# First attention block of a four-block transformer kernel: shift and scale computed in blocks of columns, and the first six projections accumulated side by side

## Chip, core and metric

One NeuronCore of a Trainium2 chip runs the whole kernel; the other cores are idle. The metric is the time of one execution in microseconds (us), taken as the median of several runs. The engines are called PE (TensorE), DVE (VectorE), ACT (ScalarE), POOL (GpSimd) and SP (SyncE, which here only issues DMAs); PEld is the loading of PE's weights.

## What is computed

The reference has four residual blocks on 1024 tokens of width 1024, in float32. Only the first is touched. Cut to what matters:

```python
mod = jax.nn.silu(c) @ ada_w[0] + ada_b[0]              # c: (1,1024), ada_w[0]: (1024, 3072)
shift, scale, gate = jnp.split(mod[:, None, :], 3, axis=-1)
u = x * (1 + scale) + shift                             # (1,1024,1024)
q, k, v, gate = jnp.split(u @ w_in, 4, axis=-1)         # w_in: (1024, 4*1152), 18 heads of 64
for g, (window, dil) in enumerate(((128, 1), (512, 4), (2048, 16))):   # 6 heads per group
    s = q k^T * 64**-0.5 + bias[t5_bucket(rel * dil)]   # masked to the dilated window
    o, lse = softmax(s) v, logsumexp(s)
y = concat(o * softmax(lse over the three groups)) * silu(gate)
x = layernorm(ALPHA * x + mod_gate * (y @ w_out))
```

Nothing can be projected before `u` is there, and a feature column of `u` needs its own shift and scale, each a product of all 1024 entries of silu(c) with one column of `ada_w`.

## The kernel before

Every float32 matrix product is made of three passes with two-part numbers: an operand is split into a rounded part `h` and a remainder `l`, and PE adds up w_l·u_h, w_h·u_h and w_h·u_l (`PASSES`). The input of a block stands transposed, by feature tiles of 128 (`kt`, eight of them) and by halves of 512 tokens (`h`): `uh0`, `ul0`, `uh1`, `ul1` (class `UT`). A projection of 128 output columns for one half of the tokens takes 8 x 3 = 24 matmuls of 512 columns into one PSUM bank.

`phase_A` is the first block. Its beginning, lines 341 to 427, goes through these steps:

- The vector `c` is loaded, turned, and passed through silu (`cs`). Four tiles of `x` (128 tokens each) are loaded on ACT's queue, then the one-hot table `oh` and `rel_bias`, from which PE forms three rows of attention biases (`tvs`). PE transposes the four `x` tiles and ACT copies them to `xT0` (`turn_x`).
- DVE forms silu(c)·ada_w for all 2048 columns of shift and scale: 16 loads of `ada_w` (128 rows x 1024 columns, in rows of 4 KB) go through the five `raw` buffers, and each is weighted by one column of `cs` and added to `acc` (lines 396 and 398).
- The first three weight tiles of `w_in` (`load_w`: columns of q, k and v for the first pair of heads) follow in SP's queue and are split on DVE. PE adds `acc` over the partitions with 16 matmuls against `cz` (32 instructions) and one transpose. `mc` then holds all 16 columns of shift and 1 + scale.
- Only now is `u` formed: per feature tile and half, DVE computes `xm`, ACT `uh`, and DVE or POOL `ul` (lines 418 to 422). The other four tiles of `x` are loaded on SP's queue behind the weights and turned.
- Three bias rows are written to DRAM and read back spread over 128 partitions (`tvd`, `tbd`), later loaded as the shifted tables `T`.

Then the groups follow. `dil_project` for the first group runs its six products (q, k, v by two halves) one after the other, each 24 matmuls into a bank of `g` or `t`, with `q`, `k` and `kl` split off PSUM by ACT and DVE while PE goes on. `dil_batches` forms the jobs of a head (ten per pair of heads): scores on PE, bias, maximum on DVE, exponential on ACT, transposes on PE (`t`), a split on ACT (`pth`) and DVE (`ptl`), and values on PE. Between the transposes and the values of a job PE is given pieces of the next group's projections (`fill`). `mod_jobs` meanwhile forms the other four slices of shift, scale and gate for later use: a load of `ada_w` and a weighing on DVE (`weigh`, line 552) per job.

The order on each engine is set by the Tile scheduler, except where `keep_in_program_order` or `self.pin` fixes it. Each engine runs its own list in order. SP's list holds nearly all DMA issues; one that waits for a buffer holds up all behind it.

Of the kernel before, what the change touches and what calls it, by code (L numbers as in the profile page):

```python
# [12 lines left out]
F32 = mybir.dt.float32  # L13
F32R = mybir.dt.float32r
I32 = mybir.dt.int32
AF = mybir.ActivationFunctionType
# [5 lines left out]
P = 128  # L22
S = 1024
D = 1024
# [117 lines left out]
class Kern:  # L142
    def __init__(self, nc, tc, ins, out):
        self.nc, self.tc, self.i, self.out = nc, tc, ins, out
        self.n = 0
        self.ready = {}
        self.pin = False
        self.ps = Pools(None, {})
# [6 lines left out]
    def tr(self, *args):  # L155
        ins = self.nc.tensor.transpose(*args)  # L156
        if self.pin:
            self.tc.keep_in_program_order(ins)

    def nm(self, s):  # L160
# [46 lines left out]

    def load_w(self, pool, w, c0, n, kts=KT, tag="w", bufs=None, dve=0, cut=1):

        nc = self.nc  # L210
        step = min(kts, max(1, 1024 // n))
        res = []
        kw = {} if bufs is None else {"bufs": bufs}
        for k0 in range(0, kts, step):
            m = min(step, kts - k0)
            r = self.raw([P, step, n])
            nc.sync.dma_start(r[:, :m], w[k0 * P:(k0 + m) * P, c0:c0 + n].rearrange("(k p) n -> p k n", p=P))
# [114 lines left out]
    def phase_A(self, x_in):  # L332
        nc, i = self.nc, self.i
        with ExitStack() as ctx:
            self.wp = self.tags(ctx, "wp", bufs=3)
# [5 lines left out]
            with ExitStack() as c0:  # L341
                tp = self.tags(c0, "a0", side="right")
                self.psum(c0, "", "mx")
                c8 = tp.tile([P, KT], F32, name="c8")
                self.transposed_columns(c8, i["c"].rearrange("o (k p) -> (o k) p", p=P), KT, tp)
                self.silu2(cs, c8, cs)
                nc.vector.tensor_scalar(cs, cs, 0.5, None, OP.mult)
                xT = [tp.tile([P, KT, 512], F32, name=f"xT{h}") for h in range(2)]

                def load_x(t):  # L350
                    xts[t] = tp.tile([P, D], F32, tag="xt", bufs=4, name=self.nm("xt"))
                    return (nc.sync if t > 3 else nc.scalar).dma_start(xts[t], x_in[t * P:(t + 1) * P, :])

                def turn_x(t):
                    xt = xts[t]
                    for h in range(2):
                        ps = self.pp("x", 3, [P, 4, P])
                        self.transposes(ps, xt[:, h * 512:(h + 1) * 512], 4)
                        dst = xT[t // 4][:, h * 4:h * 4 + 4, t % 4 * P:(t % 4 + 1) * P]
                        nc.scalar.copy(dst, ps)  # L360

                xts = {}
                for t in range(4):
                    load_x(t)

                oh = tp.tile([33, 3, 512], F32, name="oh")
                nc.scalar.dma_start(oh, i["k_onehot"])
                rb = tp.tile([33, 18], F32, name="rb")
                nc.vector.memset(rb[32:33, :], NEG)
                nc.scalar.dma_start(rb[:32, :], i["rel_bias"])  # L370
                tvs = []
                for g in range(3):
                    ps = self.pp("x", 3)
                    self.mm(ps[:6, :], rb[:, g * 6:(g + 1) * 6], oh[:, g, :], start=True, stop=True)
                    tvs.append(tp.tile([6, 512], F32, tag="tv", bufs=3, name=self.nm("tv")))
                    nc.scalar.copy(tvs[g], ps[:6, :])
# [5 lines left out]
                nc.vector.tensor_scalar(mc[:, 8:], mc[:, 8:], 1.0, None, OP.add)  # L382
                for t in range(4):
                    turn_x(t)

                cz = tp.tile([P, 256], F32, name="cz")
                nc.gpsimd.memset(cz, 0.0)
                nc.gpsimd.tensor_copy(cz[:, ::17], self.ones.to_broadcast([P, 16]))
                acc = tp.tile([P, 2, 1024], F32, name="acc")
                for kt in range(KT):  # L390
                    for j in range(2):
                        r = self.raw()
                        self.tc.keep_in_program_order(nc.sync.dma_start(
                            r, i["ada_w"][0, kt * P:(kt + 1) * P, j * 1024:(j + 1) * 1024]))
                        if kt == 0:
                            nc.vector.tensor_scalar(acc[:, j], r, cs[:, 0:1], None, OP.mult)
                        else:
                            nc.vector.scalar_tensor_tensor(acc[:, j], r, cs[:, kt:kt + 1], acc[:, j], OP.mult, OP.add)
                for c0 in (0, WA, 2 * WA):
                    self.ready[c0] = self.load_w(self.wp, i["a_w_in"][0], c0, P, dve=1 - c0)  # L400
                mp = self.pp("m", 1, [16, P])
                for c in range(16):
                    self.mm(mp, cz[:, c * 16:c * 16 + 16], acc[:, c // 8, c % 8 * P:(c % 8 + 1) * P],
                            start=(c == 0), stop=(c == 15))
                row = tp.tile([16, P], F32, name="row")
                nc.vector.tensor_copy(row, mp)
                mt = self.pp("t", 2)
                self.tr(mt[:, :16], row, self.ident[:16, :16])
                nc.vector.tensor_tensor(mc, mc, mt[:, :16], OP.add)
                for t in range(4, NT):  # L410
                    self.tc.keep_in_program_order(load_x(t))
                for h in range(2):
                    if h:
                        for t in range(4, NT):
                            turn_x(t)
                    for kt in range(KT):
                        xm = tp.tile([P, 512], F32, tag="xm", bufs=4, name=self.nm("xm"))
                        nc.vector.tensor_scalar(xm, xT[h][:, kt], mc[:, 8 + kt:9 + kt], mc[:, kt:kt + 1], OP.mult, OP.add)
                        nc.scalar.activation(ut.hi[h][:, :, kt], xT[h][:, kt], AF.Identity,
                                             bias=mc[:, kt:kt + 1], scale=mc[:, 8 + kt:9 + kt])  # L420
                        eng = nc.gpsimd if kt % 3 == 2 else nc.vector
                        eng.tensor_tensor(ut.lo[h][:, :, kt], xm.rearrange("p (t n) -> p t n", n=P),  # L422
                                          ut.hi[h][:, :, kt].bitcast(F32), OP.subtract)
                for g in range(3):
                    nc.sync.dma_start(tvd[g * 6:(g + 1) * 6, :], tvs[g])
                    nc.sync.dma_start(tbd[g * 6:(g + 1) * 6],
                                      tvd[g * 6:(g + 1) * 6, None, :].to_broadcast([6, P, 512]))
            c1 = ExitStack()
            self.psum(c1, "", "so")
            ag = self.tags(ctx, "ag")  # L430
# [18 lines left out]
            self.order += [gate_w(2, g) for g in range(3)]  # L449
            for n, _ in enumerate(fills[0]):  # L450
                self.pin = n >= 5
            mods = self.mod_jobs(lp, cs, ((0, 2), (1, 0), (1, 1), (1, 2)))
# [147 lines left out]
    def dil_project(self, lp, ut, w_in, hp, g, res):  # L600
# [15 lines left out]

        def project(c, h, evac, tag):
            w = self.next_w(c)
            self.next_w(c, 1)
            ps = self.pp(tag, 2)  # L620
# [39 lines left out]
        first = hp + g == 0  # L660
        order = [(j, h) for h in range(2) for j in range(3)]
        for j, h in order if first else sorted(order):
            yield from project(j * WA + c0, h, evacs[j], "t" if first and (j, h) == (2, 0) else "g")
        vh = lp.tile([P, NT, P], F32R, tag="vh", bufs=2, name=self.nm("vh"))
# [1241 lines left out]
```

## Time and profile before

| | |
|---|---|
| median of 3 runs | 4132.61 us (4131.44 to 4135.64) |
| the profiled execution | 4131.9 us |
| its span in the trace | 4130.1 us |
| PE busy with matmuls | 3858.2 us, 93% of the span |
| DVE, ACT, POOL busy | 59%, 33%, 26% |
| first of the 144 matmuls of the first six projections | starts at 39.80 us |
| last of them | starts at 75.72 us |
| first matmul of the second group's projections | starts at 77.53 us |

All times are from the start of the span. The span is 1.8 us shorter than the execution's own time. The last three lines of the table are read from the timeline of PE. A line such as "x<-ident,xt" names what an instruction writes and reads; "[idle before <-DVE acc]" is the time that the engine stood still ahead of it and what ended it.

### The profile page before, as it was taken

Reading aid. Unit: us, or ns where it says so; the run is one execution under the profiler, and the core shown is the slowest. Engines: PE = TensorE matmul, PEld = TensorE weight load, DVE = VectorE, ACT = ScalarE, POOL = GpSimd, SP = SyncE. Lnnn points to the kernel's source line nnn. Section 1 sums busy time; section 2 is a strip of 40 time slices with the busy share of each in tenths; the row PEclk is TensorE's granted clock in tenths of the full one; section 3 lists DMA queues with packets and bytes.
Section 4 is the critical chain, followed back from the end, with each engine's and each line's share of the span. In section 5 each row is a group of like instructions: output and inputs, shape, how many; then the busy total and the mean of one; then the engine's idle time right before and its main releaser. Section 6 shows DMA issues by size and latency. Waiting matters only on the chain. (4 is left out here: it accounts for less than half of the span.)

```text
span 4130.1 us, 54373 instructions
## 1 busy us (share of the span) xinstructions
PE 3858.2 (93%) x21085; PEld 3272.8 (79%) x21085; DVE 2447.7 (59%) x4596; ACT 1382.1 (33%) x2938; POOL 1085.5 (26%) x1016
## 2 busy tenths in 40 slices
PE   7979796899999989999999999997999999999998
PEld 5767675688889867999778888885999778888886
DVE  6645455956777767568754434338568764443436
ACT  3424242124777633256421111113136431111111
POOL 1111111420222322134233232334134232323233
PEclk9989898999999989999999999998999999999999
DMA  6363516220111243111421111113111231111112
GB/s 237 96 82 83 76 41 149 95 86 29 35 25 32 62 120 117 41 38 37 137 83 48 45 51 41 51 50 120 55 42 37 95 115 46 47 46 51 41 51 82
DMA packets 318897, 290.80 MB, mean 70 GB/s; under 512 B 70779, under 2 KB 273267, under 8 KB 318638
## 3 DMA queue, kind: packets, MB, share of 16 engines
q1 hardware_dynamic: 313362, 268.23, 23.5%
q10 hardware_dynamic: 5276, 19.08, 1.5%
q8 instruction: 167, 2.74, 0.3%
q14 instruction: 92, 0.75, 0.1%
HBM read 240.26 MB, written 51.72 MB: 71 GB/s over the span
## 5 line engine op out<-in xcount | busy, mean ns | idle before, releaser
L203 POOL TENSOR_TENSOR wl<-wr,wh 128x1024 fp32r<-128x1024 f32 (+1 forms) x253 | 495.4, 1966 | 1589.6 <-DVE wh L199 1502.8
L199 DVE CAST wh<-wr 128x1024 fp32r<-128x1024 f32 x222 | 181.9, 820 | 751.7 <-PE y L151 310.7
L151 PE MATMUL y<-uh_m,wl 128*128 128x512 f32 x1056 | 417.1, 395 | 4.7 <-DVE z L1631 4.2
L151 PE MATMUL y<-uh_m,wh 128*128 128x512 f32 x1056 | 419.8, 398 | 0.0
L151 PE MATMUL y<-ul_m,wh 128*128 128x512 f32 x1056 | 418.8, 397 | 0.0
L1784 ACT ACTIVATE cv<-y,cw 128x1024 f32<-128x1024 f32 x66 | 79.8, 1209 | 775.7 <-PE y L151 775.7
L151 PE MATMUL g<-uh_a,wl 128*128 128x512 f32 x568 | 236.8, 417 | 55.2 <-DVE sg L293 55.1
L151 PEld LDWEIGHTS y<-uh_m,wl 128*128 128x128 f32 x1056 | 199.0, 188 | 55.1 <-issue 4.6
L151 PEld LDWEIGHTS y<-uh_m,wh 128*128 128x128 f32 x1056 | 199.1, 189 | 48.4
L151 PEld LDWEIGHTS y<-ul_m,wh 128*128 128x128 f32 x1056 | 198.9, 188 | 47.6 <-DVE ul_m L191 0.9
L151 PE MATMUL y<-wo,yh 128*128 128x512 f32 x784 | 219.8, 403 | 17.0 <-ACT yh L1158 17.0
L151 PE MATMUL g<-ul_a,wh 128*128 128x512 f32 x568 | 229.3, 404 | 0.5 <-POOL ul_a L422 0.4
L151 PE MATMUL g<-uh_a,wh 128*128 128x512 f32 x568 | 228.7, 403 | 0.0
L151 PEld LDWEIGHTS y<-wo,yh 128*128 128x128 f32 x784 | 149.2, 193 | 50.7 <-ACT yh L1158 18.5
L191 DVE TENSOR_TENSOR pt<-t,pt 128x512 fp32r<-128x512 f32 x256 | 165.8, 680 | 22.2 <-ACT pt L190 20.4
L151 PE MATMUL y<-wl,hh 128*128 128x512 f32 x440 | 175.4, 399 | 0.0
L151 PE MATMUL y<-wh,hl 128*128 128x512 f32 x440 | 175.1, 398 | 0.0
L151 PE MATMUL y<-wh,hh 128*128 128x512 f32 x440 | 175.1, 398 | 0.0
L151 PEld LDWEIGHTS g<-uh_a,wl 128*128 128x128 f32 x568 | 111.5, 196 | 78.9 <-DVE sg L293 49.5
L995 DVE TENSOR_REDUCE nm<-s 128x1 f32<-128x1024 f32 x128 | 155.7, 1216 | 27.1 <-PE s L151 26.5
L151 PE MATMUL g<-wl,uh_f 128*128 128x256 f32 x576 | 166.4, 289 | 3.0 <-DVE dv L191 2.5
L151 PE MATMUL g<-wl,uh_n 128*128 128x256 f32 x576 | 166.0, 288 | 3.1 <-DVE dv L191 2.5
(446 smaller groups left out, 10312.2 us busy)
## 6 DMA issues: line engine op xcount, KB each, us to landing
wr<-w_up SPq DMA_DIRECT2D x88, 512.0 KB
wr<-ada_w SPq DMA_DIRECT2D x48, 512.0 KB
wr<-w_down SPq DMA_DIRECT2D x44, 512.0 KB
wr<-a_w_in SPq DMA_DIRECT2D x36, 512.0 KB
wr<-w_in SPq DMA_DIRECT2D x24, 512.0 KB
xs<-wr SPq DMA_DIRECT2D x16, 512.0 KB
wr<-xs ACTq DMA_DIRECT2D x16, 512.0 KB
wr<-w_in SPq DMA_DIRECT2D x32, 256.0 KB
```

The lines of the kernel that those rows point to most:

```text
L151: ins = self.nc.tensor.matmul(*args, **kw)
L191: nc.vector.tensor_tensor(lo, src, hi.bitcast(F32), OP.subtract)
L199: (self.nc.scalar.copy if act else self.nc.vector.tensor_copy)(hi, raw)
L203: (eng or self.nc.gpsimd).tensor_tensor(lo[..., cs], raw[..., cs], hi[..., cs].bitcast(F32), OP.subtract)
L995: nc.vector.tensor_reduce(nm, sp, AX.X, OP.max, negate=True)
L1784: nc.scalar.activation(t, ps, AF.Identity, bias=cw[:, 3, c:c + 1], scale=cw[:, 2, c:c + 1])
```

## The change

The beginning is written anew. Shift and scale come in four blocks of columns: block `pr` holds shift and scale of the two feature tiles 2·pr and 2·pr+1. `load_mod(pr)` loads it with eight DMAs (rows of 1 KB) into four of six new buffers `ra`; `mod(pr)` weighs it on DVE in eight steps of 512 columns, adds it over the partitions on PE with four one-column matmuls and puts it into `mc`; `modulate(kt, h)` makes `uh` and `xm` both on ACT and `ul` on DVE. `product(j, h, kts)` adds some feature tiles to projection j, half h. The six projections stand in six PSUM banks (`g`, two, and `x`, four), so that a feature tile can be added to all six as soon as it is there. The banks of the scores (`s`, `o`) are opened only after the six banks of the first group have been read (`cx.close()`). `chain` fixes the order of an engine's listed instructions; with `pin` the first three weight tiles are rounded on ACT and not on DVE.

```diff
+    def chain(self, ins):
+        prev = self.last.get(ins.ins.engine)
+        if prev:
+            self.tc.add_manual_dep(ins.ins, prev, ...)
+        self.last[ins.ins.engine] = ins.ins.name
...
-            self.wsplit(hi[:, :m], lo[:, :m], r[:, :m], eng, cut)
+            self.wsplit(hi[:, :m], lo[:, :m], r[:, :m], eng, cut, pin)
...
-                self.psum(c0, "", "mx")
+                self.psum(cx, "", "x")
+                def load_mod(pr):
+                    cols = i["ada_w"][0, :, 0:2048].rearrange("(k p) (a n) -> p k a n", p=P, a=2)
+                    rows[pr] = []
+                    for k in range(0, KT, 2):
+                        r = tp.tile([P, 2, 2, 256], F32, tag="ra", bufs=6, name=self.nm("ra"))
+                        for a in range(2):
+                            self.chain(
+                                nc.sync.dma_start(r[:, :, a], cols[:, k:k + 2, a, pr * 256:(pr + 1) * 256]))
+                        rows[pr].append(r)
+                def mod(pr):
+                    acc = tp.tile([P, 2, 256], F32, tag="acc", bufs=2, name=self.nm("acc"))
+                    for k in range(KT):
+                        r = rows[pr][k // 2][:, k % 2]
+                        self.chain(nc.vector.tensor_scalar(acc, r, cs[:, 0:1], None, OP.mult) if k == 0 else
+                                   nc.vector.scalar_tensor_tensor(acc, r, cs[:, k:k + 1], acc, OP.mult, OP.add))
+                    ps = self.pp("t", 2)[:, :4].rearrange("p (a k) -> p a k", a=2)
+                    for a in range(2):
+                        for k in range(2):
+                            self.mm(ps[:, a, k:k + 1], acc[:, a, k * P:(k + 1) * P], self.ones, start=True, stop=True)
+                    m = mc.rearrange("p (a k) -> p a k", a=2)[:, :, 2 * pr:2 * pr + 2]
+                    self.chain(nc.vector.tensor_tensor(m, m, ps, OP.add))
+                def modulate(kt, h):
+                    xm = tp.tile([P, 512], F32, tag="xm", bufs=3, name=self.nm("xm"))
+                    nc.scalar.activation(ut.hi[h][:, :, kt], xT[h][:, kt], AF.Identity,
+                                         bias=mc[:, kt:kt + 1], scale=mc[:, 8 + kt:9 + kt])
+                    nc.scalar.activation(xm, xT[h][:, kt], AF.Identity, bias=mc[:, kt:kt + 1], scale=mc[:, 8 + kt:9 + kt])
+                    self.chain(nc.vector.tensor_tensor(ut.lo[h][:, :, kt], xm.rearrange("p (t n) -> p t n", n=P),
+                                                       ut.hi[h][:, :, kt].bitcast(F32), OP.subtract))
+                for t in range(2):
+                    load_x(t, nc.scalar)
...
+                for t in (2, 3):
+                    load_x(t, nc.sync)
+                load_mod(0)
...
+                for t in range(4):
+                    turn_x(t)
+                for j in range(3):
+                    ws.append(self.load_w(self.wp, w_in, j * WA, P, dve=int(j == 1), pin=True))
+                mod(0)
+                for t in range(4, NT):
+                    load_x(t, nc.sync)
+                load_mod(1)
+                for kt in range(2):
+                    modulate(kt, 0)
+                for kt in range(2):
+                    for j in range(3):
+                        product(j, 0, [kt])
+                for t in range(4, NT):
+                    turn_x(t)
+                mod(1)
+                for kt in range(2):
+                    modulate(kt, 1)
+                load_mod(2)
+                for kt in range(2):
+                    for j in range(3):
+                        product(j, 1, [kt])
+                for kt in (2, 3):
+                    for h in range(2):
+                        modulate(kt, h)
+                mod(2)
+                load_mod(3)
+                for kt in (2, 3):
+                    for h in range(2):
+                        for j in range(3):
+                            product(j, h, [kt])
+                for kt in (4, 5):
+                    for h in range(2):
+                        modulate(kt, h)
+                mod(3)
+                for kt in (6, 7):
+                    for h in range(2):
+                        modulate(kt, h)
...
+                for kt in (4, 5):
+                    for h in range(2):
+                        for j in range(2):
+                            product(j, h, [kt])
+                for j, h in ((0, 0), (1, 0), (0, 1), (1, 1), (2, 0), (2, 1)):
+                    product(j, h, range(6 if j < 2 else 4, KT))
```

The first place is DVE's list from the second to the fourth block of columns. Here `acc` is the weighing of a block, `mc` the sum that completes its shift and scale, and `ul_a` the remainder of a feature tile, for which the two results of ACT (`xm`, `uh_a`) must be there. In the change:

```order
L392 TENSOR_TENSOR mc<-mc,t_376 128x2x2
...
L399 TENSOR_TENSOR ul_a<-xm_435,uh_a 128x4x128
L385 TENSOR_SCALAR acc_439<-ra_390,cs 128x512
L386 SCALAR_TENSOR_TENSOR acc_439<-ra_390,cs,acc_439 128x512
L386 SCALAR_TENSOR_TENSOR acc_439<-ra_393,cs,acc_439 128x512 x2
L386 SCALAR_TENSOR_TENSOR acc_439<-ra_396,cs,acc_439 128x512 x2
L386 SCALAR_TENSOR_TENSOR acc_439<-ra_399,cs,acc_439 128x512 x2
L392 TENSOR_TENSOR mc<-mc,t_448 128x2x2
L399 TENSOR_TENSOR ul_a<-xm_502,uh_a 128x4x128
...
L385 TENSOR_SCALAR acc_518<-ra_454,cs 128x512
```

Each block's weighing stands behind the last `ul_a` of the block before it (six of them ahead of `acc_439`, four ahead of `acc_518`). Before, all the weighing comes first, then one `mc`:

```order
L398 SCALAR_TENSOR_TENSOR acc<-wr_268,cs,acc 128x1024
L199 CAST wh_276<-wr_271 128x1024
...
L409 TENSOR_TENSOR mc<-mc,t_317 128x16
L418 TENSOR_SCALAR xm_331<-xT_111,mc 128x512
L418 TENSOR_SCALAR xm_335<-xT_111,mc 128x512
L418 TENSOR_SCALAR xm_339<-xT_111,mc 128x512
L422 TENSOR_TENSOR ul_a<-xm_331,uh_a 128x4x128
```

The second place is DVE's list in the eighth and ninth of the ten jobs of the first group. Here `xs`, `stats` and `ptl` are a job's biased scores, maximum and split remainder; `wr<-wr,cs,wr` is a weighing of `mod_jobs`. Before:

```order
L762 SCALAR_TENSOR_TENSOR xs_1075<-s_1070,T_715 128x512
L191 TENSOR_TENSOR ptl_1086<-t_1080,pth_1085 128x512
L769 TENSOR_REDUCE stats_717<-xs_1075 128x2
L552 SCALAR_TENSOR_TENSOR wr_760<-wr_1067,cs,wr_760 128x1024
L762 SCALAR_TENSOR_TENSOR xs_1128<-s_1123,T_715 128x512
L769 TENSOR_REDUCE stats_717<-xs_1128 128x2
L191 TENSOR_TENSOR ptl_1139<-t_1133,pth_1138 128x512
```

In the change:

```order
L829 TENSOR_REDUCE stats_743<-xs_1101 128x2
L609 SCALAR_TENSOR_TENSOR wr_786<-wr_834,cs,wr_786 128x1024
L609 SCALAR_TENSOR_TENSOR wr_786<-wr_881,cs,wr_786 128x1024
L609 SCALAR_TENSOR_TENSOR wr_786<-wr_931,cs,wr_786 128x1024
L207 CAST wh_952<-wr_950 128x1024
L609 SCALAR_TENSOR_TENSOR wr_786<-wr_1001,cs,wr_786 128x1024
L609 SCALAR_TENSOR_TENSOR wr_786<-wr_1046,cs,wr_786 128x1024
L207 CAST wh_1117<-wr_1115 128x1024
L609 SCALAR_TENSOR_TENSOR wr_786<-wr_1093,cs,wr_786 128x1024
L822 SCALAR_TENSOR_TENSOR xs_1154<-s_1149,T_741 128x512
L829 TENSOR_REDUCE stats_743<-xs_1154 128x2
L199 TENSOR_TENSOR ptl_1165<-t_1159,pth_1164 128x512
```

Six weighings and two roundings of weights now stand in a row between the eighth job's maximum and the ninth job's scores; before, the six were spread over the third to the ninth job. On PE the two lists are the same, instruction for instruction, from the first group's v transposes to the end; on DVE, ACT, POOL and SP they are the same from the tenth job of the first group.

## Rows read from the trace of the kernel before

**Rows 1.** The page's first part: busy us, share of the span, instructions.
```profile
PE 3858.2 (93%) x21085; PEld 3272.8 (79%) x21085; DVE 2447.7 (59%) x4596; ACT 1382.1 (33%) x2938; POOL 1085.5 (26%) x1016
```
**Rows 2.** Windows: engines' busy us, then granted clock, DMA share, GB/s.
```profile
0.00:4.00 4.00, 0.24 (x1) 0.18 (x1) 0.30 (x3) 0.00 (x0) 1.11 (x8) 1.00 0.54 150
4.00:8.00 4.00, 0.28 (x1) 0.18 (x1) 0.68 (x4) 1.49 (x2) 0.00 (x0) 1.00 1.02 418
8.00:12.00 4.00, 0.00 (x0) 0.00 (x0) 1.50 (x2) 0.00 (x0) 0.00 (x0) 1.00 1.03 370
12.00:16.00 4.00, 1.51 (x2) 0.24 (x3) 2.03 (x2) 0.00 (x0) 0.00 (x0) 1.00 1.03 362
...
32.00:36.00 4.00, 4.00 (x24) 2.98 (x23) 3.59 (x4) 0.00 (x0) 0.00 (x0) 0.61 1.15 321
```
**Rows 3.** Timeline of PE: start us, us, instruction [idle before].
```profile
14.48 5.28 PE L151 MATMUL x<-oh,rb 33*6 33x512 f32 x6 [9.44 <-DMA rb<-rel_bias]
19.69 6.24 PE L156 MATMUL x<-ident,xt 128*128 128x128 f32 x32
30.71 5.81 PE L151 MATMUL m<-acc,cz 128*16 128x128 f32 x32 [4.78 <-DVE acc L398]
...
39.80 0.50 PE L151 MATMUL g<-uh_a,wl 128*128 128x512 f32 x1 [0.16 <-ACT uh_a L419]
...
46.95 1.47 PE L156 MATMUL x<-ident,xt 128*128 128x128 f32 x12
```
**Rows 4.** Timeline of PE, end of the first six projections and after.
```profile
75.50 0.39 PE L151 MATMUL g<-uh_a,wh 128*128 128x512 f32 x1
75.72 0.40 PE L151 MATMUL g<-ul_a,wh 128*128 128x512 f32 x1
...
77.53 0.45 PE L151 MATMUL g<-uh_a,wl 128*128 128x512 f32 x1
...
82.60 0.75 PE L156 MATMUL t<-ident,xs 64*128 64x64 f32 x2 [1.63 <-ACT xs L771]
...
84.73 0.63 PE L151 MATMUL g<-uh_a,wl 128*128 128x512 f32 x1
85.16 0.63 PE L151 MATMUL g<-uh_a,wh 128*128 128x512 f32 x1
```
**Rows 5.** Timeline of ACT.
```profile
25.10 1.56 ACT L360 COPY xT<-x 128x512 f32<-128x512 f32 x3 [0.25 <-PE x L156]
...
38.92 5.76 ACT L419 ACTIVATE uh_a<-xT,mc 128x512 fp32r<-128x512 f32 x8
54.69 1.17 ACT L634 CAST q<-g 64x512 fp32r<-64x512 f32 x2
```
**Rows 6.** Groups by line and shape, ACT: count | busy us, mean ns.
```profile
L1797 ACT CAST hh<-cv 128x1024 fp32r<-128x1024 f32 x44 | 46.2, 1049 | 172.8 <-DVE cv L1794 172.8
```
**Rows 7.** Groups by line and shape, 0 to 60 us, DVE.
```profile
L398 DVE SCALAR_TENSOR_TENSOR acc<-wr,cs,acc 128x1024 f32<-128x1024 f32 x14 | 17.9, 1285 | 2.6 <-DMA wr<-ada_w 2.6
...
L422 DVE TENSOR_TENSOR ul_a<-xm,uh_a 128x512 fp32r<-128x512 f32 x12 | 7.9, 682 | 0.1
...
L199 DVE CAST wh<-wr 128x1024 fp32r<-128x1024 f32 x3 | 2.1, 688 | 0.5 <-DMA wr<-a_w_in 0.5
```
**Rows 8.** Timeline of DVE, the first group's splits.
```profile
66.48 1.39 DVE L636 TENSOR_TENSOR q<-g,q 64x512 fp32r<-64x512 f32 x2 [0.52 <-ACT q L634]
71.92 2.81 DVE L647 TENSOR_TENSOR kl<-g,k 64x512 fp32r<-64x512 f32 x4 [4.05 <-ACT k L644]
```
**Rows 9.** Timeline of POOL: splitting the second group's first weights.
```profile
66.04 2.40 POOL L203 TENSOR_TENSOR wl<-wr,wh 128x1024 fp32r<-128x1024 f32 x1 [9.53 <-DVE wh L199]
```
**Rows 10.** Waits, 77 to 135 us: engine <- releaser: us, times, longest.
```profile
PE o L151 <- DVE ptl L191: 3.1, 4, 1.3
...
DVE wh L199 <- DMA wr<-a_w_in: 2.8, 1, 2.8
...
PE o L151 <- ACT pth L190: 1.7, 1, 1.7
```

More of the change, by code (lines that the diff above doesn't have):

```diff
@@ L145, in __init__ @@
         self.n = 0
-        self.ready = {}
+        self.ready, self.last = {}, {}
         self.pin = False
@@ L342, in phase_A, with load_x @@
                 tp = self.tags(c0, "a0", side="right")
-                self.psum(c0, "", "mx")
+                self.psum(cx, "", "x")
+                xT = [tp.tile([P, KT, 512], F32, name=f"xT{h}") for h in range(2)]
+                w_in = i["a_w_in"][0]
+                xts, ws, rows, done = {}, [], {}, set()
+                def load_x(t, eng):
+                    xts[t] = tp.tile([P, D], F32, tag="xt", bufs=4, name=self.nm("xt"))
+                    self.chain(eng.dma_start(xts[t], x_in[t * P:(t + 1) * P, :]))
@@ L344, in phase_A, with product @@
+                def product(j, h, kts):
+                    if (j, h) not in self.first:
+                        self.first[j, h] = self.pp(*(("g", 2) if len(self.first) < 2 else ("x", 4)))
+                    self.gemm_T_half(ws[j], ut, h, self.first[j, h], kts=kts)
+                for t in range(2):
+                    load_x(t, nc.scalar)
                 c8 = tp.tile([P, KT], F32, name="c8")
@@ L347, in phase_A @@
                 nc.vector.tensor_scalar(cs, cs, 0.5, None, OP.mult)
[L348 to L367, printed above, removed]
                 rb = tp.tile([33, 18], F32, name="rb")
                 nc.vector.memset(rb[32:33, :], NEG)
[L370 to L376, printed above, removed]
+                self.chain(nc.scalar.dma_start(rb[:32, :], i["rel_bias"]))
+                oh = tp.tile([33, 3, 512], F32, name="oh")
+                self.chain(nc.scalar.dma_start(oh, i["k_onehot"]))
                 self.ones = self.cp.tile([P, 1], F32, name="ones")
@@ L382, in phase_A @@
                 nc.vector.tensor_scalar(mc[:, 8:], mc[:, 8:], 1.0, None, OP.add)
+                for t in (2, 3):
+                    load_x(t, nc.sync)
+                load_mod(0)
+                self.first = {}
+                self.pin = True
+                tvs = []
+                for g in range(3):
+                    ps = self.pp("t", 2)
+                    self.mm(ps[:6, :], rb[:, g * 6:(g + 1) * 6], oh[:, g, :], start=True, stop=True)
+                    tvs.append(tp.tile([6, 512], F32, tag="tv", bufs=3, name=self.nm("tv")))
+                    nc.scalar.copy(tvs[g], ps[:6, :])
@@ L383, in phase_A @@
                 for t in range(4):
                     turn_x(t)
[L386 to L407, printed above, removed]
@@ L408, in phase_A @@
-                self.tr(mt[:, :16], row, self.ident[:16, :16])
-                nc.vector.tensor_tensor(mc, mc, mt[:, :16], OP.add)
-                for t in range(4, NT):
[L411 to L423, printed above, removed]
@@ L424, in phase_A @@
[L424 to L427 removed]
+                for j in range(3):
+                    ws.append(self.load_w(self.wp, w_in, j * WA, P, dve=int(j == 1), pin=True))
+                    self.ready[j * WA] = ws[j]
+                mod(0)
+                for t in range(4, NT):
+                    load_x(t, nc.sync)
@@ new lines, in phase_A @@
+                for g in range(3):
+                    self.chain(nc.sync.dma_start(tvd[g * 6:(g + 1) * 6, :], tvs[g]))
+                    self.chain(nc.sync.dma_start(
+                        tbd[g * 6:(g + 1) * 6], tvd[g * 6:(g + 1) * 6, None, :].to_broadcast([6, P, 512])))
+                for kt in (4, 5):
+                    for h in range(2):
+                        for j in range(2):
+                            product(j, h, [kt])
+                for j, h in ((0, 0), (1, 0), (0, 1), (1, 1), (2, 0), (2, 1)):
+                    product(j, h, range(6 if j < 2 else 4, KT))
@@ L449, in phase_A @@
             self.order += [gate_w(2, g) for g in range(3)]
-            for n, _ in enumerate(fills[0]):
-                self.pin = n >= 5
+            for _ in fills[0]:
+                pass
+            cx.close()
+            self.psum(c1, "", "so")
             mods = self.mod_jobs(lp, cs, ((0, 2), (1, 0), (1, 1), (1, 2)))
@@ L615, in dil_project, with project @@
         out = res[hp * 3 + g] = []
-        def project(c, h, evac, tag):
+        def project(c, h, evac):
             w = self.next_w(c)
             self.next_w(c, 1)
-            ps = self.pp(tag, 2)
+            if first:
+                evac(h, perm(self.first.pop((c // WA, h))))
+                return
+            ps = self.pp("g", 2)
             for k0 in (0, 4):
@@ L660, in dil_project @@
         first = hp + g == 0
-        order = [(j, h) for h in range(2) for j in range(3)]
+        order = [(0, 0), (1, 0), (0, 1), (1, 1), (2, 0), (2, 1)]
         for j, h in order if first else sorted(order):
-            yield from project(j * WA + c0, h, evacs[j], "t" if first and (j, h) == (2, 0) else "g")
+            yield from project(j * WA + c0, h, evacs[j])
         vh = lp.tile([P, NT, P], F32R, tag="vh", bufs=2, name=self.nm("vh"))
```

14 lines of the change are left out of this document (11 added, 3 removed).

## Prediction

> **What bounds the kernel now.** Read the page's first part to begin with [rows 1]: PE is busy for 93% of the span, so a delay of PE's own list lasts to the end. From the first group's v transposes on, PE's list is the same in both programs, and nothing later in it is due at a fixed time. So the question is when PE gets there, and what the other engines' lists, which differ as far as the group's tenth job, make it wait for.
>
> Next the windows [rows 2]: from 4 to 16 us the DMA engines are full at 360 to 420 GB/s while PE does next to nothing. Then the timeline of PE [rows 3, 4]: bias rows from 14.48 us, transposes of x, the sum of shift and scale at 30.71, the first projection at 39.80, and 144 matmuls until 75.96 (0.227 us each, from the spacing of the last two), with transposes between. The second group starts at 77.53. Until 39.80 PE has little to do; that is the room the change aims at.
>
> **The change, step by step.** Times are from the start of the span.
>
> *Bias rows.* They wait for the one-hot table behind four x tiles on ACT's queue: 2.3 MB. By 14.48 us both queues have moved 0.6 + 1.67 + 1.48 + 0.9 = 4.65 MB [rows 2], twice 2.3, so they share evenly. Two x tiles fewer leave 1.25 MB, hence 2.5 MB in all: 8.6 us. I take **9**; bounds 7 (the table needs no share) and 11 (the rate falls to 362 GB/s while they land).
>
> *First half of x.* 5.2 us of bias rows, then eight transposes with copies, 19.69 to 26.66 [rows 3, 5]: 7.0. On ACT, three roundings of weights now stand between the copies: 1.05 each [rows 6], of which I take 2.4 as added (none to 3.2). x is ready at **23.6**. Block 1's sums are done by then: its 2.1 MB follow the 2.3 MB of the start, 4.4 MB by 14 us; the weights' 1.6 MB follow by 18.5, in time for their roundings.
>
> *First 18 products.* Two ACT results at 0.72 [rows 5] and one remainder at 0.68 [rows 7] come first: 25.7. Then 16 matmuls: 3.6 us at 0.227. [...] I add 1.7: **31.0**.
>
> [...]
>
> *Second half of x.* Its four loads wait on SP for the buffers of the first four tiles, and block 2's eight loads stand behind them. They are issued between 15 and 22 us and land by 25, hidden. Eight transposes, 6.0 (7.0 at the low level, 5 where only ACT's copies count): xT1 is complete at **37.0**.
>
> *Block 3.* ACT makes 12 results, 8.6 us. The last remainder, 0.7. Only then does DVE weigh block 3, since it stands behind the remainders in its list: one step of 0.4 and seven of 0.64 (half of the 1.285 for twice the columns [rows 7]), 4.9. The sum: four matmuls, two instructions each at 0.18 [rows 3], and the addition, 1.7 (1.1 to 2.5). **52.9**. The loads are there: two blocks, 4.2 MB, in the 25 us since. PE has had 18 products and stands idle from about 42.
>
> *Block 4.* ACT 8 results, 5.8; remainder 0.7; weighing 4.9; sum 1.7: 13.1, so **66.0**. PE's 36 products of feature tiles 2 and 3 take 8.2 and lie inside, low clock included.
>
> *The rest.* 24 products of tiles 4 and 5 and 48 more stand behind block 4's sum in PE's list: 72 x 0.227 = 16.3. ACT's last results (5.8 after the sum) lie under the first 24. PE was idle for some 2 us; after 1.63 us at 82.60 seven matmuls took 0.43 [rows 4], so 1.7 for the clock (0 to 4). **84.0**, against 75.96: **+8.0**.
>
> *Tail.* The second group's first weights are rounded on DVE behind all of q's and k's splits (8.4 us, twice 1.39 and twice 2.81 [rows 8]; they begin 8.3 us before PE's end, since the first product is complete 42 matmuls or 9.5 us before it and ACT needs 1.17 [rows 5]), then 0.7 and POOL's 2.4 [rows 9]: 3.2 after PE's end, where it was 1.6. **+1.6**. The v copies and the later opening of the score banks end about 2 us after PE's end, under that. The tables T come last in SP's list, after block 4; they wait for freed memory until about 72 us and are wanted after 88, so they cost nothing; should they be late, a load and DVE's step.
>
> *Jobs.* Six weighings at 1.28 and two roundings at 0.69 hold DVE for 9.1 us between the eighth and ninth job; with the ninth's scores and maximum the eighth's remainder comes 11.1 us late (bias 0.69, maximum 0.68, split 0.68). PE has about 4.7 us to do meanwhile (exponential, transposes, 12 matmuls). It waits 6.4, up to 9.2 where a weight load lands late as before (2.8 [rows 10]). Gained back: weighings leave the earlier jobs, where PE waited 3.1 for DVE and 1.7 for ACT behind it [rows 10]. I take half of the 3.1, bounds none and 4.8. **+5** (1.6 to 9.2).
>
> *Removed or moved at no cost:* 32 instructions of the old sum on PE and 16 `xm` on DVE lie in the stretch that is rebuilt; POOL's four remainders go to DVE, counted above.
>
> Sum, against the profiled execution's 4131.9 (0.7 under the median of 4132.6, well inside the runs' spread): 4131.9 + 8.0 + 1.6 + 5 = 4146.5, say **4147**. A measurement of this kernel can tell 0.2%, 8.3 us, from no change. The bounds: all low ends together (start -2, roundings -2.4, both clocks -3.4, two sums -1.2, jobs -3.4) give 4134; that they all fall together is unlikely, so 4136. All high ends (start +2, roundings +0.8, clock +2.3, sums +1.6, jobs +4.2) give 4157, and 1.7 more where the long wait among the jobs lowers the clock as that at 82.60 did: 4159.
>
> **Rivals.**
>
> *The jobs lose nothing.* PE would need 11 us of other work between the eighth job's maximum and its values; then the weighings' leaving the earlier jobs counts in full: 4131.9 + 9.6 - 4.8 = 4136.7, no slower than can be told. For it: PE has pieces of projections to fill with. Against: 12 matmuls, 2.7 us, stand there in its list. 13%.
>
> *The blocks overlap after all.* If DVE weighed the next block while ACT works on this one, each block would cost the longer of the two, at most 7.6 (four remainders and a weighing) instead of 13 to 16, and the loads would decide. The 14.2 MB of x, weights and `ada_w` at 370 GB/s end near 40, plus 3 of weighing and sum, plus 16.3: PE done at 60, 16 earlier: 4131.9 - 16 + 1.6 + 5 = 4122.5, faster. It decides once weighing does not wait for remainders; DVE's list says it does. 5%.
>
> [...] 15%.
>
> **Chances.** My forecast 67%, the three rivals 13, 5 and 15%. The forecast's lower end and the first rival make the middle: slower by over 0.2% 0.80, within 0.2% 0.15, faster 0.05. The range 4136 to 4159 holds the forecast with its bounds, the low-clock rival and most of the first.
>
> **What would show it.** In the changed profile: bias rows from about 9 us; DVE's third and fourth block each begin right after a remainder; PE idle for some 10 us before block 3's sum; the last of the six products near 84 and the second group's first matmul near 87; one wait of PE for `ptl` of 6 us or more. Wrong, if PE's first six projections end before 76 us, or if no `ptl` wait passes 3 us.

## The result, and the profile after it

The changed kernel takes 4160.1 us (median of 6 runs, 4158.2 to 4164.1) against 4134.2 us for the kernel before on the same chip: a ratio of 1.0064 (95% interval 1.0051 to 1.0077), so 26 us slower. The forecast was 4147 us, at most 4159. The direction was right and the size too small: the start cost 4 us more than forecast, the jobs three times as much as forecast. The profiled span is 4158.8 us, 28.7 more than before. The page's first part [rows 1] hardly shows it, since PE does the same work:

```profile
PE 3864.8 (93%) x21084; PEld 3277.8 (79%) x21084; DVE 2445.1 (59%) x4597; ACT 1396.9 (34%) x2957; POOL 1083.6 (26%) x1012
```

**The start.** The windows of the changed kernel (columns as in [rows 2]) show PE idle twice, each time with the granted clock down to 0.50 behind it:

```profile
44.00:48.00 4.00, 0.82 (x4) 0.34 (x2) 3.02 (x5) 1.56 (x3) 0.00 (x0) 0.84 0.00 0
48.00:52.00 4.00, 0.00 (x0) 0.00 (x0) 3.82 (x6) 0.00 (x0) 0.00 (x0) 0.50 0.69 215
52.00:56.00 4.00, 3.66 (x13) 3.30 (x14) 0.39 (x3) 1.59 (x3) 0.00 (x0) 0.50 0.24 86
...
64.00:68.00 4.00, 1.04 (x7) 1.07 (x7) 2.70 (x4) 0.00 (x0) 0.00 (x0) 0.90 0.35 108
68.00:72.00 4.00, 4.00 (x12) 3.23 (x13) 1.09 (x3) 3.21 (x5) 0.00 (x0) 0.50 0.43 146
```

DVE's timeline tells why. Block 3 is weighed from 46.21 us, right after the remainder of 45.60; its sum is in `mc` at 54.38, and only then may ACT go on. Block 4's is there at 68.76. The forecast had 52.9 and 66.0:

```profile
45.60 0.69 DVE L399 TENSOR_TENSOR ul_a<-xm,uh_a 128x512 fp32r<-128x512 f32 x1 [0.72 <-ACT xm L398]
46.21 0.48 DVE L385 TENSOR_SCALAR acc<-ra,cs 128x512 f32<-128x512 f32 x1
46.72 5.47 DVE L386 SCALAR_TENSOR_TENSOR acc<-ra,cs,acc 128x512 f32<-128x512 f32 x7
54.22 0.16 DVE L392 TENSOR_TENSOR mc<-mc,t 128x4 f32<-128x4 f32 x1 [2.02 <-PE t L151]
...
68.60 0.16 DVE L392 TENSOR_TENSOR mc<-mc,t 128x4 f32<-128x4 f32 x1 [1.79 <-PE t L151]
```

The timeline of PE gives the places that the prediction named [rows 3, 4]: bias rows at 9.42 us (forecast 9), the matmuls that add up blocks 3 and 4 from 52.34 and 66.96, the second group's first matmul at 91.15 (forecast near 87), where it was 77.53:

```profile
9.42 5.28 PE L151 MATMUL t<-oh,rb 33*6 33x512 f32 x6 [4.25 <-DMA oh<-k_onehot]
14.63 4.70 PE L156 MATMUL t<-ident,xt 128*128 128x128 f32 x20
19.71 1.14 PE L156 MATMUL t<-ident,xt 128*128 128x128 f32 x8 [0.38 <-ACT xT L367]
...
24.73 0.40 PE L151 MATMUL g<-uh_a,wh 128*128 128x512 f32 x1
26.05 0.64 PE L151 MATMUL g<-ul_a,wh 128*128 128x512 f32 x1 [0.92 <-DVE ul_a L399]
...
52.34 1.84 PE L151 MATMUL t<-ones,acc 128*128 128x1 f32 x8 [7.53 <-DVE acc L386]
66.96 1.60 PE L151 MATMUL t<-ones,acc 128*128 128x1 f32 x8 [3.11 <-DVE acc L386]
...
91.15 0.79 PE L151 MATMUL g<-uh_a,wl 128*128 128x512 f32 x1 [0.50 <-POOL wl L211]
...
131.43 0.60 PE L156 MATMUL t<-ident,xs 128*128 128x128 f32 x4
143.63 0.79 PE L151 MATMUL g<-uh_a,wl 128*128 128x512 f32 x1 [11.61 <-POOL wl L211]
144.22 0.63 PE L151 MATMUL g<-uh_a,wh 128*128 128x512 f32 x1
```

**The jobs.** The last three lines are the surprise. After the transposes of 131.43 us PE stands still for 11.61 us, and the twelve matmuls behind that run at the lower clock, 0.43 apart, with 0.50 granted from 140 to 148 us. PE waits for the second group's third weights (v). DVE rounds them only from 140.41, behind three weighings, and POOL's remainder follows from 141.24. Of the 11.6 us, DVE's list up to the eighth job's maximum takes 4.6, the weighings 3.8, the rounding 0.8 and POOL 2.4:

```profile
136.58 3.92 DVE L609 SCALAR_TENSOR_TENSOR wr<-wr,cs,wr 128x1024 f32<-128x1024 f32 x3
140.41 0.69 DVE L207 CAST wh<-wr 128x1024 fp32r<-128x1024 f32 x1
```

The table of waits, 90 to 160 us, has that wait, and next to nothing of the wait on `ptl` that the prediction was built on [rows 10]:

```profile
PE g L151 <- POOL wl L211: 12.1, 2, 11.6
PE o L151 <- DVE ptl L199: 1.5, 2, 0.9
```

The weights themselves had been there for long. The timeline of SP's queue shows their load issued at 94.88 us, and after it nothing for 43 us:

```profile
81.18 10.76 SPq L599 DMA_DIRECT2D wr<-ada_w  x3
94.88 0.38 SPq L225 DMA_DIRECT2D wr<-a_w_in  x1
137.88 0.33 SPq L599 DMA_DIRECT2D wr<-ada_w  x1
```

The waits of SP say what it stood for, a row buffer that a weighing had not yet freed (all three waits of this kind together 43.5 us):

```profile
SPq L599 <- DVE wr L609: 43.5, 3, 42.5
```

In windows of 10 us, DMA share and GB/s are the last two columns. The changed kernel:

```profile
100.00:110.00 10.00, 9.34 (x61) 7.71 (x60) 6.08 (x9) 4.36 (x12) 0.00 (x0) 1.00 0.01 2
110.00:120.00 10.00, 10.00 (x70) 8.57 (x69) 3.49 (x6) 3.66 (x9) 0.00 (x0) 1.00 0.00 0
120.00:130.00 10.00, 7.36 (x31) 5.58 (x31) 5.01 (x12) 4.64 (x13) 0.00 (x0) 0.83 0.00 0
130.00:140.00 10.00, 2.02 (x18) 1.60 (x16) 7.90 (x10) 4.00 (x9) 0.00 (x0) 0.77 0.09 21
```

and the kernel before, which never stops transferring there:

```profile
100.00:110.00 10.00, 8.33 (x50) 6.64 (x48) 6.98 (x12) 3.29 (x7) 0.00 (x0) 1.00 0.31 83
110.00:120.00 10.00, 8.01 (x45) 6.15 (x46) 7.17 (x15) 4.93 (x15) 3.40 (x1) 1.00 0.29 70
120.00:130.00 10.00, 9.04 (x63) 7.51 (x62) 8.82 (x13) 5.11 (x14) 0.43 (x1) 1.00 0.42 133
```

**Where the 28.7 us arose.** PE's list is the same in both programs from the second group on, so each of its matmuls, counted from the end, can be set against itself. The second group begins 13.6 us late (91.15 against 77.53). The matmul that stands at 100.1 us before is 13.7 late, that of 131.2 us 27.3, that of 200.2 us 29.3, the end 28.7. So the start costs 13.6 (forecast 9.6), the jobs up to 200 us 15.7 (forecast 5), the rest next to nothing. Of the 15.7, the stop is about 11.5, the twelve matmuls behind it 2.4, and 2.0 come late, at 217 us, where PE waits 1.64 us for `vl` and seven matmuls behind that start 0.42 to 0.58 apart, with 0.87 granted from 210 to 220 us.

### The profile page after: what moved, and what is told of

It is laid out like the page before. It is cut to its first block, busy times and chain, and to the rows that moved or that the text cites. A ratio compares the mean times of both kernels' runs of the same rounds, so it can differ in the third digit from the quotient of the medians.

```text
span 4158.8 us, 54393 instructions
## 1 busy us (share of the span) xinstructions
PE 3864.8 (93%) x21084; PEld 3277.8 (79%) x21084; DVE 2445.1 (59%) x4597; ACT 1396.9 (34%) x2957; POOL 1083.6 (26%) x1012
## 5 line engine op out<-in xcount | busy, mean ns | idle before, releaser
L151 PEld LDWEIGHTS y<-wo,yh 128*128 128x128 f32 x784 | 149.1, 193 | 51.0 <-ACT yh L1218 18.9
```

The costliest lines, as they stand in the source:

```text
L151: ins = self.nc.tensor.matmul(*args, **kw)
```

## The experiments

Two losses, two questions. For the start: do the serial steps of a block decide (theory), or the loads? For the jobs: is it the v weights' rounding behind weighings, or the weighings' own time in front of `ptl`, as predicted? After four runs a third theory was needed. The runs were made in three sets, each beside the kernel before on the same chip (4120.0, 4133.6 and 4120.7 us), so ratios are compared. "Group 2" is the start of the second group's first matmul; "jobs" is what is lost from there to the matmul that stands at 200.2 us before. Both come from the profiles and are set against the one profile of the kernel before that is shown here. The two profiles of the change itself, with a0, differ by 4.4 us in the last column, most of it slow matmuls behind waits of under 2 us (in the change, eight start 0.42 to 0.59 apart behind a wait of 0.50 us at 91.15, and seven behind 1.64 us at 217.25; in a0, behind 0.51 and 1.25 us, the same ones start 0.23 to 0.34 apart), so smaller differences tell nothing.

| run | ratio to the kernel before | group 2, us | jobs, us |
|---|---|---|---|
| the kernel before | 1 | 77.5 | 0 |
| the change | 1.0064 (1.0051 to 1.0077) | 91.2 | 15.7 |
| a0, the change again | 1.0069 (1.0056 to 1.0081) | 90.4 | 11.3 |
| e4, start woven | 1.0043 (1.0029 to 1.0056) | 79.0 | 13.3 |
| e1, weighings to group 2 | 1.0084 (1.0070 to 1.0098) | 87.8 | 21.4 |
| e2, v weights first | 1.0050 (1.0038 to 1.0063) | 90.9 | 12.2 |
| e6, rounding alone | 1.0062 (1.0049 to 1.0075) | 91.1 | 12.9 |
| e7, weighings spread | 1.0055 (1.0042 to 1.0067) | 90.5 | 6.5 |
| e10, weighings as before | 1.0037 (1.0025 to 1.0049) | 91.0 | 1.2 |
| e13, before, weighings held | 1.0024 (1.0016 to 1.0033) | 78.0 | 12.1 |
| e8 = e4 + e7 | 1.0021 (1.0012 to 1.0031) | 80.0 | 8.0 |
| e11 = e4 + e10 | 1.0006 (0.9998 to 1.0015) | 80.2 | 2.2 |
| e9 = e8 + products ahead | 1.0034 (1.0022 to 1.0047) | 80.2 | 9.0 |
| e12 = e11 + products ahead | 1.0019 (1.0011 to 1.0028) | 80.3 | 3.8 |

### The start: e4

`mod` is cut into `weigh` and `total`, and both are woven into the block before:

```diff
+                for kt in (2, 4):
+                    pr = kt // 2 + 1
+                    modulate(kt, 0)
+                    weigh(pr, 0, 3)
+                    modulate(kt, 1)
+                    weigh(pr, 3, 6)
...
+                    modulate(kt + 1, 0)
+                    weigh(pr, 6, KT)
+                    total(pr)
+                    modulate(kt + 1, 1)
```

> At the start, the weighing of block 3 is set between block 2's remainders on DVE (and block 4's between block 3's), and the sum of a block stands on PE between the products of two feature tiles. Theory (a block's weighing, 6 us, stands behind the remainders of the block before, and ACT waits for its sum): the first six projections end at 68 to 72 us instead of 87.5, and the time falls by 15 to 19 us, to 4141 to 4145. Rival (the loads of the rows, or PE's products at the lower clock, set the pace): they end at 82 or later, and less than 6 us is gained, 4154 or more. The stop at 132 us after the span's start is untouched and comes correspondingly earlier.

The last of the six products starts at 75.13 us instead of 87.28, and the second group at 78.97. So the order of DVE's list was what cost the time, and no load: 12.2 us of the 13.6 are back. The run's own forecast, an end at 68 to 72 us and 15 to 19 us less, was missed: the ratio falls by 0.0021, some 9 us. DVE needs 10.5 us for a block (sum to sum, 49.63 to 60.15), and not the 8.8 of four remainders (0.69 each) and a weighing (6.0). PE's timeline still has the stop of the jobs, 12 us earlier and just as long, as expected:

```profile
59.09 1.02 PE L151 MATMUL t<-ones,acc 128*128 128x1 f32 x8 [2.56 <-DVE acc L389]
...
131.44 0.79 PE L151 MATMUL g<-uh_a,wl 128*128 128x512 f32 x1 [11.61 <-POOL wl L211]
```

### The jobs: e1, e2 and e6

e1 takes no step of `mod_jobs` in the first group and two per job in the second:

```diff
-                    next(mods, None)
+                    for _ in range((0, 2)[j] if j < 2 else 1):
+                        next(mods, None)
```

> The steps that weigh rows of the next layers' scale and shift are taken out of the first group's jobs (the second group takes two per job instead). Both theories, that the stop at 132 us comes from the weights' rounding queued behind weighings and that it comes from the weighings in front of the jobs' own splits, expect the stop of 11.6 us to go, with the 2.4 us that the 12 matmuls behind it lose at the lower clock: 12 to 14 us below the changed kernel's 4160.1, so 4146 to 4148 us, ratio to the kernel before about 1.003. If the stop stays, it has nothing to do with the weighings (a load, or a bank of PSUM).

The stop at 132 us is gone, but the run is no faster than the change (1.0084 against 1.0064, with intervals that overlap): the doubled weighings cost the second group waits of 3.29 us, 7.13 us (both for `ptl`) and 4.63 us (`vl`) at 178 to 219 us. The loss moved with the weighings.

e2 asks for the v weights ahead of the first job, one line behind `self.psum(c1, "", "so")`:

```diff
+            self.next_w(2 * WA + 384)
```

> One line: the second group's third set of weights is asked for ahead of the first job, so that its rounding stands on DVE ahead of all weighings. Theory (the rounding was queued behind three weighings): PE's wait on POOL's remainder of these weights is gone, no other wait over 3 us takes its place up to 150 us, and the time falls by 12 to 14 us to 4146 to 4148. Rival (the load of these weights, or PE's wait on the jobs' splits, sets the end of this stretch): less than 4 us is gained, 4156 or more.

Both theories missed. The weights' wait is gone, and PE stops three times 10 to 16 us later instead, the third time for the third group's weights. Its timeline:

```profile
153.71 2.24 PE L156 MATMUL t<-ident,wr 128*128 128x128 f32 x8 [3.13 <-ACT wr L719]
...
158.49 0.69 PE L156 MATMUL t<-ident,xs 128*128 128x128 f32 x2 [1.68 <-DVE vl L199]
160.09 0.79 PE L151 MATMUL g<-uh_a,wl 128*128 128x512 f32 x1 [0.91 <-POOL wl L211]
```

The first of them leads to ACT, which copies v into a row buffer (`vt` is one of the five) and had waited for one that still held a row of `ada_w`. The profile names that row's load; the fifth weighing of a run on DVE ends at 153.00, just ahead of it:

```profile
153.07 1.07 ACT L719 COPY wr<-g 128x512 f32<-128x512 f32 x2 [7.57 <-DMA wr<-ada_w]
```

e6 moves that rounding alone, to ACT at about 124 us, and holds the second weighing behind the eighth job's maximum, as the change has it:

```diff
+        c = (self.nc.scalar.copy if act or early else self.nc.vector.tensor_copy)(hi, raw)
+        if early:
+            self.chain(c)
...
+                if kern.jobs == 8:
+                    for w in kern.held:
+                        kern.tc.add_manual_dep(w.ins, red.ins.name, ...)
```

> The rounding of those weights alone is moved, to ACT at about 124 us; the weighings stay held behind the eighth job's maximum on DVE, in a run ahead of the later jobs' splits, as in the changed kernel. Theory: the wait of 11.6 us on the weights is gone and only the wait on a split that the prediction had (3 to 6 us) is left; the time falls by 8 to 10 us, to 4150 to 4152. Rival (the weighings' own time on DVE and their loads hold the jobs): the wait moves to the jobs' splits at nearly its full length, and less than 3 us is gained, 4157 or more.

The wait for the weights is gone, `ptl` costs one wait of 2.23 us, and 4.29 us for `vl` come at 161 us. Nothing worth naming is won: the rounding decides where PE stops, not that it stops.

### A third theory: e7, e10 and e13

The five row buffers stay full: in the change one takes the running sum, three hold rows that DVE has not weighed, and the fifth the v weights that it has not rounded. SP's queue stops at the next load (the 42.5 us above), and with it everything behind: the third group's weights, the next rows, the buffer for v. e7 sets each weighing ahead of the scores of the job after next:

```diff
+            if slot == 0:
+                self.held[self.jobs + 2] = w
...
+                w = kern.held.pop(kern.jobs, None)
+                if w is not None:
+                    kern.tc.add_manual_dep(first[0].ins, w.ins.name, ...)
```

> Nothing is moved to another engine and no load is asked for earlier; each weighing of the first group's jobs is only made to stand on DVE ahead of the scores of the job after next, so they no longer stand in a run. New theory (the five row buffers stay full of unweighed rows, SP's queue stands still behind them, and the weights that come next are late): the transfers go on between 100 and 135 us, the stop of 11.6 us is gone and no other over 3 us follows up to 200 us; PE is 12 to 15 us ahead of the changed kernel at the end of the second group's values, the ratio to the kernel before falls from 1.0064 to 1.003 to 1.0035. Rival (each weighing costs the jobs its 1.3 us wherever it stands): the stop goes, but 7 waits of about 1 us take its place and the ratio stays above 1.005.

A miss, by its edit. The scheduler did not bring the weighing forward but put the scores back: the second weighing starts at 121.53 us, SP's next load at 122.84, and PE waits for a job's exponential:

```profile
125.48 0.69 PE L156 MATMUL t<-ident,xs 128*128 128x128 f32 x2 [7.06 <-ACT xs L839]
```

e10 fixes each weighing where the kernel before has it: nothing that a later step puts on DVE (scores, `ptl`, the splits of q and k) may pass it:

```diff
+    def after(self, ins):
+        if self.gate:
+            self.tc.add_manual_dep(ins.ins, self.gate, ...)
...
+            self.gate = w.ins.name if slot == 0 and kt < KT - 1 else None
...
+            self.after(nc.vector.tensor_tensor(lo, src, hi.bitcast(F32), OP.subtract))
```

> The changed kernel with every weighing of the first group's jobs fixed on DVE where the kernel before has it: one between the eighth weight column's jobs, ahead of all that the next job puts there. The run before this one of the same aim let the weighings slip 15 us and only moved the stop. Theory (full row buffers, SP's queue standing still): transfers go on between 100 and 135 us, no wait of PE over 3 us from 95 to 200 us, PE 12 to 14 us ahead of the changed kernel from 150 us on; ratio 1.003 to 1.0037. Rival (a weighing costs its 1.3 us wherever it stands, or the late loads of the start reach into the jobs): 1.005 or more.

As expected: no wait of PE is over 1.8 us between 98 and 200 us, the jobs lose 1.2 us, and the windows show transfers again:

```profile
110.00:120.00 10.00, 9.06 (x62) 7.38 (x61) 4.84 (x8) 4.11 (x11) 2.40 (x1) 1.00 0.41 105
120.00:130.00 10.00, 7.97 (x45) 6.08 (x42) 6.66 (x12) 3.91 (x10) 0.66 (x1) 1.00 0.36 100
```

e13 is the counter-test: the kernel *before*, with its weighings held as the change holds them.

```diff
+                if kern.jobs == 8:
+                    kern.tc.add_manual_dep(kern.held.ins, red.ins.name, ...)
```

> The kernel before, with one thing changed: the second to eighth weighings of its jobs are held on DVE behind the eighth job's maximum. The v weights' rounding stays where it is, early. Theory (row buffers full of unweighed rows stop SP's queue): transfers stop for 25 to 35 us, PE loses 9 to 14 us in waits between 115 and 150 us although nothing of the start is touched, ratio 1.0022 to 1.0034. Rival (the stop needs the rounding of the v weights in the run, or the changed start): under 4 us, ratio below 1.001.

It loses 12.1 us in the jobs, with nothing of the start touched and the v weights rounded early. So the late weighings are the cause. In its windows the transfers run dry and come back once DVE has weighed:

```profile
100.00:110.00 10.00, 8.76 (x52) 7.03 (x50) 5.61 (x11) 2.87 (x7) 0.00 (x0) 1.00 0.12 21
110.00:120.00 10.00, 8.59 (x38) 6.99 (x39) 2.04 (x5) 4.54 (x14) 0.00 (x0) 0.66 0.02 2
120.00:130.00 10.00, 8.13 (x49) 6.38 (x47) 9.71 (x13) 3.75 (x10) 0.00 (x0) 1.00 0.26 76
```

The full buffers are not the whole way from the weighings to PE, though. The 12.1 us arise in three places, each with slow matmuls behind its wait, 0.43 apart from 114.31 to 117.73, 134.24 to 135.52 and 147.89 to 152.16 us (granted clock 0.66, 0.83 and 0.79 in the windows of 110 to 120, 130 to 140 and 140 to 150):

```profile
111.28 0.27 PE L151 MATMUL o<-pth,vl 128*64 128x128 f32 x1 [2.52 <-ACT pth L190]
131.64 0.27 PE L151 MATMUL o<-ptl,vh 128*64 128x128 f32 x1 [2.24 <-DVE ptl L191]
145.63 0.69 DVE L199 CAST wh<-wr 128x1024 fp32r<-128x1024 f32 x1 [2.72 <-DMA wr<-a_w_in]
146.98 0.69 PE L156 MATMUL t<-ident,xs 128*128 128x128 f32 x2 [4.39 <-DVE vl L191]
```

The first (1.73 us in the kernel before) brings 1.5 us of the loss and the second 4.1. The second is weighings ahead of a split on DVE, as the prediction had it. The third brings 6.5: the split of v stands behind roundings of weights that came late, in a row that begins with a load issued at 129.22 us, where the kernel before issues it at 109.75. e6 shows the same two last waits (2.23 and 4.29). So about half of the loss goes through SP's queue. More row buffers, which would part this half from the rest, were not tried.

### Both together, and one step further: a0, e8, e11, e9, e12

> The changed kernel again, unedited, on the chip of the following runs: a ratio of 1.005 to 1.008 to the kernel before, and the same stop of 11 to 12 us on the third weights of the second group at about 132 us.

It came as expected, with a wait of 11.60 us.

> The woven start and the spread weighings together. If the two losses are separate and these are all there is, both go: PE is within 2 us of the kernel before from the second group on, ratio 1.000 to 1.0012. If one of them hides behind the other, the ratio stays above 1.003.

> The woven start with the weighings of the jobs fixed as in the run before. If the two losses are all there is: PE within 2 us of the kernel before from 150 us on, ratio 1.000 to 1.001. If something else of the change costs time in the jobs: 1.002 or more.

e8 has e7's fault and keeps 8.0 us of loss in the jobs; its ratio lies between its two forecasts. e11 has neither loss but a start 2.7 us late, and its ratio of 1.0006 cannot be told from 1: together the two make up the whole of it, and, as far as the intervals tell, they add.

e9 and e12 fill the wait ahead of block 4's sum, which is 2.56 us in e4 at 59.09 and 0.92 in the profiles of e8 and e11:

```diff
-                        for j in range(3 if kt == 2 else 2):
+                        for j in range(3):
...
-                    product(j, h, range(6 if j < 2 else 4, KT))
+                    product(j, h, range(6, KT))
```

> As the run before it, and the third projection's products of feature tiles 4 and 5 stand ahead of the last block's sum as well, so that PE has 6 matmuls (1.4 us) more in the stretch of 2.6 us in which it waited for that sum. Theory: the wait falls to about 1.2 us and the 9 matmuls behind it keep the higher clock (0.23 instead of 0.43 each): 2 to 3 us less than that run, ratio 0.9993 to 1.0007. Rival: the clock falls all the same, or the last 36 products wait for the last remainders instead; the same time as that run within 1 us.

> As the run before, with the third projection's products of feature tiles 4 and 5 ahead of the last block's sum. The start ends 2 to 3 us earlier than in that run; if the second group's first weights are in time, all of it is kept (0.9993 to 1.0003), and if they are not (as in the run of the same start before), PE waits for them and 1 us or nothing is kept.

The wait is gone in both, and the last product starts at 73.7 us, 2.4 to 2.7 earlier than without it. Nothing of it reaches the second group, which starts at 80.2 to 80.3 us as before, so e9's forecast was missed and e12's second case came. Its first weights are rounded on DVE behind the splits of q and k (77.04 us in e12, 76.96 in e11), which start when the first banks are complete, and that is no earlier (68.57 us in e12, 68.50 in e11). Both ratios are 0.0013 above those of e8 and e11, at the edge of what the intervals can tell; PE has two waits more there, 2.5 and 1.5 us at 78 and 80 us. What order of the splits would use the earlier end was not tried. No version beat the kernel before.

## Why the prediction was right and wrong

- **The serial chain of the blocks: right.** Weighing behind the last remainder, ACT waiting for the sum and PE for both, PE idle before block 3's sum (7.5 us, forecast some 10): all seen, and e4 shows it by taking the order away. The first products end at 31.4 us (31.0), the second half of x is there at 37.1 (37.0).
- **The clock of the first products: right in size, its source not shown.** No run shows the 1.7 us added to the first 18 products as a term of its own; it was the author's estimate. What the change shows in its place: eight of these products stand 0.43 apart and the later ones 0.23, some 1.6 us more, with 0.78 and 0.79 granted from 24 to 28 and 28 to 32 us. They did not begin slow: the transposes took 0.235 us each from 14.63 and 0.14 from 19.71, the second matmul 0.40 (those 0.43 apart are 0.63 long), and the matmuls went to 0.43 behind two waits of 1.25 and 0.92 us. In the kernel before, too, the transposes change pace: the last seven of the 32 that begin at 19.69 us stand 0.11 apart, those ahead of them 0.21. The granted clock reads 1.00 across both paces (12 to 24 us in the change, 16 to 28 in the kernel before), so what slowed the transposes is not shown. The "7.0 at the low level" for the second half of x is not shown as a clock level either: in the change its transposes and copies took from 31.39 to 37.1 us, with 1.00 granted from 32 to 36.
- **Its size: 3.5 us too small, 87.5 against 84.0.** The term that failed is "one step of 0.4 and seven of 0.64 (half of the 1.285 ...), 4.9". A weighing took 6.0 us (46.21 to 52.19): seven steps of 0.78. That is 2.2 us over both blocks, in a term for which the prediction gave no bounds. The sum took 2.2 and 2.0 us, not 1.7, and the last 72 products 18.7, not 18.0.
- **The tail:** 3.6 us after PE's end, forecast 3.2, with the mechanism named (rounding behind the splits).
- **The jobs: the run of weighings was seen, its effect mistaken.** The failed step is "hold DVE for 9.1 us between the eighth and ninth job; ... the eighth's remainder comes 11.1 us late". It priced a weighing as DVE time, and of what is queued behind it on DVE it looked at `ptl` alone. The longest wait for `ptl` was 0.9 us. The run also held a rounding that was counted (0.69 us) without asking who waits for it, and that is where PE stood in the change, for 11.6 us. With that rounding early (e6, e13) the loss is about as large: each weighing not done keeps a row buffer, so SP's queue stands still and later weights come late, and PE waits 2.2 us for `ptl` besides. That "weighings leave the earlier jobs" was booked as a gain, and was the cause of the loss: 15.7 us in place of 5 (e10 and e13).
- **Rivals.** That the jobs lose nothing, and that the blocks overlap, are out. Nor did the clock stay low until the last 72 products: the windows grant 1.00 from 32 to 36 and from 60 to 64 us, and what the stretches at 0.50 cost lies inside the measured terms. By the prediction's own test ("if no `ptl` wait passes 3 us") its mechanism in the jobs is wrong.

## To carry to other kernels

When an instruction slips later in an engine's list, ask what it sets free, not only what stands behind it. A consumer of a ring of buffers that slips stops the queue that fills the ring, and every load behind that one, however little time the consumer takes itself: here seven steps of 1.3 us, held together, stopped SP's queue for 42.5 us in the change and cost the jobs 11 to 16 us, in e13 about half of it through late loads. And where an order comes out of a scheduler, a change in one stage can move it in the next (why it did here is not shown); fixing the order there won the lost time back for a few lines.

## What was not expected of the hardware

- A dependent step of 512 columns on DVE takes 0.78 us (5.47 for seven) where one of 1024 takes 1.28 (17.9 for 14 [rows 7]): halving the columns saves 39%. By their difference a fixed part of about 0.28 us would be in each, an estimate from these two times alone; the forecast's half of the longer one had only half of it.
- The same 72 products behind block 4's sum took 17.3, 18.9 or 20.5 us from the sum's start to their end, after idle stretches of PE of 1.74 us (e1), 2.53 and 2.91 (e7, a0) and 2.99 to 3.12 (e2, e6, e10 and the change): some 1.3 us more of waiting went with three more of matmuls. No run varied that wait alone, so the wait as the reason is not shown. In the change, with 0.50 granted from 68 to 72 us, a dozen of them stand 0.43 apart.
